# First gate columns of a decoder layer's FFN: low weights meet both token tiles at once, row statistics squared on VectorE

## The chip, the cores and the metric

The kernel runs on one core of one Trainium2 chip. The metric is the device time of one execution in microseconds; several runs are made and their median is compared.

## The reference, cut to what matters

One hybrid decoder layer over 256 tokens of 2048 columns, all float32. Two attention groups share one input projection; their normalised outputs go through one output projection; then comes a GeGLU MLP with a causal depthwise convolution between the up-projection and the activation. The place of the change is the seam between the two sub-layers:

```python
mix = jnp.concatenate([o_a, o_b], axis=-1) @ w_out[l]
x = x + rmsnorm(mix, post_mix_g[l])
h = rmsnorm(x, pre_ffn_g[l])
u = causal_dwconv(h @ w_up[l], conv_w[l], conv_b[l])
gate, val = jnp.split(u, 2, axis=-1)
y = (jax.nn.gelu(gate, approximate=True) * val) @ w_down[l]
```

So the mean square of a whole row of `mix` (2048 columns) must be known before that row's residual can be formed, and the whole residual row is needed, transposed, before the first columns of `h @ w_up` are complete.

## The kernel before, in words

**Tiles.** Tokens are two tiles of 128 rows (0 and 1). A matmul operand is kept as a high part in a reduced format and a low part, the rest; a product is high times high, high times low and low times high. `hT` holds the FFN's input transposed: for each of 16 k tiles of 128 columns, 256 columns with the high part of both token tiles and 256 with the low part. A matmul of high weights streams high and low input together (512 columns for both token tiles, or 2 x 128 for one); a matmul of low weights streams the high input alone (256 columns for both tiles, 128 for one).

**Weights** come in units of 512 KB. The SP queue loads a unit into one of five `raw` buffers, ScalarE casts it to the high part (L95, L112), VectorE subtracts that from `raw` to make the low part (L98, L115). The low split is the last reader of `raw`, so it frees the buffer for the load five units later. A projection of 256 columns takes four units of four k tiles each. `proj_T4` multiplies the high parts of units one and two, their low parts, the low parts of units three and four, and the high parts of these last.

**The seam.** The output projection's last 1024 columns (column blocks 2 and 3) are made tile by tile. A block is added to `mix` on VectorE (`evac_b`, L736), squared and summed on ScalarE (L737) and multiplied by the gain on GpSimd (L738). When all of a tile's sums are there, `mix_rstd` reduces them on VectorE and raises to -0.5 on GpSimd (L183); four `residual` steps on VectorE (L756) make the residual row. `turn` transposes 512 columns of it on PE (L763), writes the high parts of `hT` on ScalarE (`high`, L768) and the low parts on VectorE (`low`, L773). Tile 0 is finished while PE still multiplies tile 1's last output columns.

**`first_gate`** multiplies the first 256 gate columns in two passes, tile 0 while tile 1's residual row is made, then tile 1. Its four weight units are split ahead of it (`gate_unit`); `lows` holds the low splits of units two, three and four, which are called where the code puts them. Before the change, the low weights of units one and two meet tile 0 and tile 1 apart (128 columns each, L928), those of units three and four meet both together (256 columns, L928).

**What sets the order.** PE runs in the order of the program throughout. ScalarE, VectorE and GpSimd run in the order of the program from the output projection's last blocks to the end of `first_gate`; work outside it (casts and splits of the following units, the convolution) is placed into their queues by a scheduler when the program is built. After `first_gate` come the first 256 value columns (`proj_T4`), then the second 256 gate columns, and beside these the convolution of the finished columns: ScalarE copies (L897), VectorE adds (L898), GpSimd multiplies with the row factors `rowf` (L899), ScalarE and VectorE apply the three taps (L901, L903, L905), ScalarE the activation, VectorE the product with the value columns (L1075) and the sums for later use (L958 to L961). The row factors need the FFN's row statistics: squares of the residual rows on ScalarE (L782), a diagonal on VectorE (L203), a matmul that spreads it (L209) and a copy (L866).

Of the kernel before, what the change touches and what calls it, by code (L numbers as in the profile page):

```python
# [8 lines left out]
F32 = mybir.dt.float32  # L9
F32R = mybir.dt.float32r  # L10
BF16 = mybir.dt.bfloat16
AF = mybir.ActivationFunctionType
ALU = mybir.AluOpType
# [4 lines left out]
P = 128  # L18
# [13 lines left out]
def hybrid_layer(ctx: ExitStack, tc: tile.TileContext, x, pre_mix_g, w_in, b_forget, sinks,  # L32
# [282 lines left out]
    with tc.tile_pool(name="mixp", bufs=1) as mp:  # L315
# [416 lines left out]
        def evac_b(t, n, b, h=None):  # L732
            i, cs = (n, slice(0, 512)) if h is None else (4 if h else n,
                                                          slice(h * 256, h * 256 + 256))
            m = mix[t][n][:, cs]
            dve.scalar_tensor_tensor(m, b[:, cs], rstd_b[t], m, op0=ALU.mult, op1=ALU.add)  # L736
            act.activation(junk[:, cs], m, AF.Square, accum_out=msq[t][:, i:i + 1])  # L737
            pool.tensor_tensor(m, m, gbc[:, n * 512:(n + 1) * 512][:, cs], op=ALU.mult)  # L738
# [10 lines left out]
        def mix_rstd(t):  # L749
            st = small.tile([P, 1], F32, tag="st", name="st_m")  # L750
            dve.tensor_reduce(st, msq[t][:, 0:4 + t], axis=AX.X, op=ALU.add)
            rmix.append(rstd_of(st, D, f"rmix{t}"))

        def residual(t, n):
            xs = x_sb[:, t, n * 512:(n + 1) * 512]
            dve.scalar_tensor_tensor(xs, mix[t][n], rmix[t], xs, op0=ALU.mult, op1=ALU.add)  # L756

        def turn(t, n):

            tb = bank("att")  # L760
            for j in range(4):
                c = n * 512 + j * P
                pe.transpose(tb[:, j * P:(j + 1) * P], x_sb[:, t, c:c + P], ident)  # L763
            kts = [(n * 4 + j, tb[:, j * P:(j + 1) * P]) for j in range(4)]

            def high():
                for kt, b in kts:
                    act.activation(hT[:, kt, t * P:(t + 1) * P], b, AF.Copy,  # L768
                                   scale=gcol[:, 16 + kt:17 + kt])

            def low():
                for kt, b in kts:
                    dve.scalar_tensor_tensor(hT[:, kt, 256 + t * P:256 + (t + 1) * P], b,  # L773
                                             gcol[:, 16 + kt:17 + kt],
                                             hT[:, kt, t * P:(t + 1) * P].bitcast(F32),
                                             op0=ALU.mult, op1=ALU.subtract)

            return high, low
# [6 lines left out]
        def out_cols(n, t, cs):  # L785
            b = bank()
            for k, hi, lo in kept[n]:
                mm3(b[:, cs], oT[8 + k], t, hi, lo, cs, k == 0, k == 7)
            return b
# [40 lines left out]
        lows[0]()  # L830
        for _, low in turns:
            low()
        evac_b(1, 2, out_cols(2, 1, slice(0, 256)), 0)
        lows[1]()
        turns = [turn(0, 2), turn(0, 3)]
        for high, _ in turns:
            high()
        turns[0][1]()
        evac_b(1, 2, out_cols(2, 1, slice(256, 512)), 1)
        turns[1][1]()  # L840
        mix_rstd(1)
        for n in range(4):
            residual(1, n)
        hold.__exit__(None, None, None)

# [1 line left out]
    with tc.tile_pool(name="ffn", bufs=1) as fp:  # L847
# [61 lines left out]
        def first_gate():  # L909

            banks = [bank(), bank()]

            def one(t, u):
                ts = slice(t * P, t * P + P)

                both = u >= 2
                ls = slice(0, 256) if both else ts

                def v(x):
                    return x.rearrange("p (h t c) -> p h t c", h=2, t=2)[:, :, t, :]  # L920

                for low in (False, True)[:1 if both and t == 0 else 2]:
                    for kt in range(u * 4, u * 4 + 4):
                        hi, lo = gate[kt]
                        for m, b in enumerate(banks):
                            ms = slice(m * P, (m + 1) * P)
                            if low:
                                pe.matmul(b[:, 256 + ls.start:256 + ls.stop], lo[:, ms],  # L928
                                          hT[:, kt, ls], start=False,
                                          stop=(t == 1 and kt == KT - 1))  # L930
                            else:
                                pe.matmul(v(b), hi[:, ms], v(hT[:, kt, :]),  # L932
                                          start=(t == 0 and kt == 0), stop=False)

            one(0, 0)
            one(0, 1)
            one(0, 2)
            for high, low in [turn(1, u) for u in range(4)]:
                high()
                low()  # L940
            one(0, 3)
            lows[2]()
            x_squares(0)
            x_squares(1)
            for t in range(2):
                act.dma_start(x_dram[t * P:(t + 1) * P, :], x_sb[:, t, :])
            rows = ffn_tables()
            for u in range(4):
                one(1, u)
            later(1, rows)  # L950
            return banks

# [294 lines left out]
```

## Time and profile before

| what | value |
|---|---|
| median of 3 runs | 1063.57 us (1063.05, 1063.57, 1065.51) |
| span of the profiled execution | 1062.6 us; no other time is listed for it |
| mean granted TensorE clock | 0.996 |
| busy: PE, VectorE, ScalarE, GpSimd | 1049.6, 839.7, 639.1, 229.3 us |
| the seam, 333.2 to 348.0 us: PE, VectorE, ScalarE, GpSimd busy | 14.80, 13.27, 10.38, 1.43 us of 14.80 |

Times are microseconds from the span's start. PE, DVE, ACT, POOL and SP are TensorE, VectorE, ScalarE, GpSimd and the DMA queue of SyncE. A row of the timeline has start, length, engine, line, operation, operands and count, and in brackets the idle time before it and what ended it. Successive instructions of an engine overlap a little, so a row's length is somewhat more than what it adds. The chain of waits goes by ends, so its rows for PE start 0.16 us later than the same work in the timeline.

### The profile page before, as it was taken

The numbers are of one execution on the slowest core, as the hardware profiler recorded it, in microseconds if no ns is written. First come the engines' busy times: TensorE is split into PE (matmuls) and PEld (weight loads), VectorE is DVE, ScalarE is ACT, GpSimd is POOL, SyncE is SP. The second block draws the span as 40 slices with busy tenths as digits, with TensorE's granted clock in tenths as the row PEclk, the third lists the DMA queues.
The fourth block names the chain that finished last, engine by engine and source line by source line (L and its number), as shares of the span: only waits on it lengthen the run. The fifth ranks groups of instructions, "written<-read, shape, count | busy, mean of one in ns | idle before, by whom it ended". The sixth has DMA issues, their size and how long they took to land.

```text
span 1062.6 us, 16272 instructions
## 1 busy us (share of the span) xinstructions
PE 1049.6 (99%) x5890; PEld 914.6 (86%) x5890; DVE 839.7 (79%) x1369; ACT 639.1 (60%) x1096; POOL 229.3 (22%) x256
## 2 busy tenths in 40 slices
PE   9999999999999999999999999999999999999996
PEld 7889988888889888888888888888888888888885
DVE  5988887887467887787767999668778687789987
ACT  6767667776556765566655556446556565556551
POOL 4253335441022121211212000002121121200004
PEclk9999999999999999999999999999999999999998
DMA  8745566555773876656665666666566665656563
GB/s 280 217 120 168 162 209 202 165 170 162 282 236 107 280 231 187 193 180 185 211 188 188 193 204 206 213 196 190 169 209 188 197 197 180 194 179 200 194 242 121
DMA packets 154285, 207.08 MB, mean 195 GB/s; under 512 B 6845, under 2 KB 131037, under 8 KB 153181
## 3 DMA queue, kind: packets, MB, share of 16 engines
q1 hardware_dynamic: 153200, 203.37, 60.7%
q10 hardware_dynamic: 1004, 2.68, 0.6%
q8 instruction: 46, 0.75, 0.3%
q14 instruction: 35, 0.28, 0.1%
HBM read 201.68 MB, written 4.21 MB: 194 GB/s over the span
## 4 chain that ended last, share of the span: by engine, by line
PE 84%; DVE 9%; issue 2%; DMA 2%; ACT 2%; POOL 1%; DVEq 0%; SPq 0%; POOLq 0%; ACTq 0%
PE bank_acc L284 15%; PE bank_att L284 14%; PE bank_acc L309 12%; PE bank_att L967 9%; PE bank_acc L290 8%; PE bank_att L290 7%; PE bank_acc L253 7%; DVE wlo L313 4%; PE bank_acc L258 4%; PE bank_acc L967 2%; PE bank_att L475 1%; PE bank_att L510 1%; DVE wlo L115 1%; PE bank_acc L932 1%; DMA raw<-in_w_down_dram 1%
## 5 line engine op out<-in xcount | busy, mean ns | idle before, releaser
L115 DVE TENSOR_TENSOR wlo<-raw,whi 128x1024 fp32r<-128x1024 f32 (+3 forms) x271 | 328.5, 1224 | 127.0 <-ACT whi L112 118.4
L112 ACT CAST whi<-raw 128x1024 fp32r<-128x1024 f32 (+3 forms) x270 | 273.2, 1029 | 131.8 <-issue 88.8
L899 POOL TENSOR_TENSOR room<-room,rowf 128x256 f32<-128x256 f32 x88 | 100.3, 1160 | 393.9 <-DVE room L898 392.0
L284 PE MATMUL bank_acc<-hT,whi 128*128 128x512 f32 x736 | 173.3, 390 | 0.0
L284 PEld LDWEIGHTS bank_acc<-hT,whi 128*128 128x128 f32 x736 | 136.4, 188 | 27.4
L967 PE MATMUL bank_att<-whi,G 128*128 128x512 f32 x488 | 156.0, 389 | 0.0
L284 PE MATMUL bank_att<-hT,whi 128*128 128x512 f32 x640 | 150.6, 390 | 0.0
L284 PEld LDWEIGHTS bank_att<-hT,whi 128*128 128x128 f32 x640 | 118.7, 188 | 23.9
L967 PEld LDWEIGHTS bank_att<-whi,G 128*128 128x128 f32 x488 | 91.6, 188 | 18.9
L967 PE MATMUL bank_att<-wlo,G 128*128 128x512 f32 x244 | 95.0, 389 | 0.2 <-DVE wlo L313 0.2
L290 PEld LDWEIGHTS bank_acc<-hT,wlo 128*128 128x128 f32 x736 | 89.3, 188 | 2.0
L290 PE MATMUL bank_acc<-hT,wlo 128*128 128x256 f32 x736 | 89.8, 279 | 0.0
L901 ACT ACTIVATE room<-room,cw 128x256 f32<-128x256 f32 x88 | 53.0, 602 | 60.6 <-POOL room L899 60.6
L253 PE MATMUL bank_acc<-hT,whi 128*128 128x512 f32 x352 | 88.0, 395 | 0.0
L309 PE MATMUL bank_acc<-whi,oT 128*128 128x512 f32 (+1 forms) x272 | 81.7, 379 | 0.0
L290 PEld LDWEIGHTS bank_att<-hT,wlo 128*128 128x128 f32 x640 | 77.6, 188 | 1.7
L290 PE MATMUL bank_att<-hT,wlo 128*128 128x256 f32 x640 | 77.9, 279 | 0.0
L903 DVE SCALAR_TENSOR_TENSOR room<-room,cw 128x256 f32<-128x256 f32 x88 | 62.4, 709 | 17.6 <-ACT room L901 17.3
L253 PEld LDWEIGHTS bank_acc<-hT,whi 128*128 128x128 f32 x352 | 63.3, 188 | 11.5
L313 DVE TENSOR_TENSOR wlo<-raw,whi 128x1024 fp32r<-128x1024 f32 (+1 forms) x56 | 61.3, 1119 | 12.1 <-ACT whi L312 12.1
L312 ACT CAST whi<-tb 128x1024 fp32r<-128x1024 f32 x42 | 44.0, 1050 | 43.0 <-PE bank_att L967 19.6
L312 ACT CAST whi<-raw 128x1024 fp32r<-128x1024 f32 (+1 forms) x56 | 52.3, 958 | 27.1 <-PE bank_att L967 20.6
(254 smaller groups left out, 1594.0 us busy)
## 6 DMA issues: line engine op xcount, KB each, us to landing
raw<-in_w_up_dram SPq DMA_DIRECT2D x176, 512.0 KB, 4.2
raw<-in_w_down_dram SPq DMA_DIRECT2D x58, 512.0 KB, 4.7
raw<-in_w_in_dram SPq DMA_DIRECT2D x51, 512.0 KB, 4.7
raw<-in_w_out_dram SPq DMA_DIRECT2D x32, 512.0 KB, 4.6
extra<-in_w_down_dram SPq DMA_DIRECT2D x20, 512.0 KB, 4.7
raw<-in_w_in_dram SPq DMA_DIRECT2D x16, 384.0 KB, 3.6
tb<-in_w_down_dram SPq DMA_DIRECT2D x10, 512.0 KB, 3.5
cb<-c_dram SPq DMA_DIRECT2D x8, 256.0 KB, 3.8
```

What stands on the lines that cost most here:

```text
L112: i1 = act.copy(hi[:, cs], raw[:, cs])
L115: i2 = dve.tensor_tensor(lo[:, cs], raw[:, cs], hi[:, cs].bitcast(F32), op=ALU.subtract)
L253: pe.matmul(b, parts[u][0][:, a, m * P:(m + 1) * P], hT[:, kt, :], start=(kt == 0), stop=(kt == KT - 1))
L284: pe.matmul(b, parts[u][0][:, a, m * P:(m + 1) * P], hT[:, kt, :], start=(kt == 0), stop=(kt == KT - 1))
L290: pe.matmul(b[:, 256:512], parts[u][1][:, a, m * P:(m + 1) * P], hT[:, kt, 0:256], start=False, stop=False)
L309: pe.matmul(b, a, r[:, cols], start=(first and i == 0), stop=(last and i == 2))
L312: act.copy(hi, src)
L313: dve.tensor_tensor(lo, src, hi.bitcast(F32), op=ALU.subtract)
L899: pool.tensor_tensor(u[:, 2:258], u[:, 2:258], rowf, op=ALU.mult)
L901: act.activation(y, u[:, 2:258], AF.Identity, bias=cw[:, 3, ch:ch + 1], scale=cw[:, 2, ch:ch + 1])
L903: dve.scalar_tensor_tensor(y, u[:, 1:257], cw[:, 1, ch:ch + 1], y, op0=ALU.mult, op1=ALU.add)
L967: pe.matmul(b[:, to] if to else b, a, r[:, cols], start=(first and i == 0), stop=(last and i == 2))
```

## The change

In `first_gate`, tile 0 now meets the high weights alone. All low weights meet both tiles together, 256 columns at a time, each unit's right behind its high weights' pass over tile 1. Tile 1's transposes move: blocks 0 and 1 ahead of tile 0's fourth high unit, blocks 2 and 3 behind it. The low splits of gate units three and four move behind tile 1's low parts of blocks 2 and 3.

In the row statistics of tile 1, ScalarE squares the first half of column block 2 between the high parts of tile 0's blocks 2 and 3; the sums so far are reduced on VectorE into `v`; the second half is added, then squared and summed on VectorE (`tensor_tensor_reduce`, an operation that the kernel has elsewhere in another form, L481), and the power follows on GpSimd. The gain of that half is multiplied on GpSimd behind the power, and the residual of block 2 is made last.

```diff
+        def mix_others():
+            st = small.tile([P, 1], F32, tag="st", name="st_m")
+            dve.tensor_reduce(st, msq[1][:, 0:4], axis=AX.X, op=ALU.add)
+            v = small.tile([P, 1], F32, tag="rv", name="rv")
+            dve.tensor_scalar(v, st, 1.0 / D, EPS, op0=ALU.mult, op1=ALU.add)
+            return v
+        def square_b(t, n, h):
+            m = mix[t][n][:, h * 256:h * 256 + 256]
+            act.activation(junk[:, 0:256], m, AF.Square, accum_out=msq[t][:, n:n + 1])
+            pool.tensor_tensor(m, m, gbc[:, n * 512 + h * 256:n * 512 + h * 256 + 256],
+                               op=ALU.mult)
...
-        evac_b(1, 2, out_cols(2, 1, slice(0, 256)), 0)
-        lows[1]()
+        b12 = out_cols(2, 1, slice(0, 256))
+        dve.scalar_tensor_tensor(mix[1][2][:, 0:256], b12[:, 0:256], rstd_b[1], mix[1][2][:, 0:256],
+                                 op0=ALU.mult, op1=ALU.add)
         turns = [turn(0, 2), turn(0, 3)]
-        for high, _ in turns:
-            high()
-        turns[0][1]()
-        evac_b(1, 2, out_cols(2, 1, slice(256, 512)), 1)
-        turns[1][1]()
-        mix_rstd(1)
-        for n in range(4):
+        turns[0][0]()
+        square_b(1, 2, 0)
+        turns[1][0]()
+        for _, low in turns:
+            low()
+        v = mix_others()
+        b12 = out_cols(2, 1, slice(256, 512))
+        m12 = mix[1][2][:, 256:512]
+        dve.scalar_tensor_tensor(m12, b12[:, 256:512], rstd_b[1], m12, op0=ALU.mult, op1=ALU.add)
+        ms = small.tile([P, 1], F32, tag="rv", name="ms")
+        dve.tensor_tensor_reduce(junk[:, 256:512], m12, m12, 1.0 / D, v, ALU.mult, ALU.add, ms)
+        r12 = small.tile([P, 1], F32, tag="rmix1", bufs=2, name="rmix1")
+        pool.tensor_tensor(r12, ms, mhalf, op=ALU.pow)
+        rmix.append(r12)
+        pool.tensor_tensor(m12, m12, gbc[:, 1280:1536], op=ALU.mult)
+        for n in (0, 1, 3, 2):
             residual(1, n)
...
-            one(0, 0)
-            one(0, 1)
-            one(0, 2)
-            for high, low in [turn(1, u) for u in range(4)]:
+            def v(x, t):
+                return x.rearrange("p (h t c) -> p h t c", h=2, t=2)[:, :, t, :]
+            def highs(t, u):
+                for kt in range(u * 4, u * 4 + 4):
+                    for m, b in enumerate(banks):
+                        pe.matmul(v(b, t), gate[kt][0][:, m * P:(m + 1) * P], v(hT[:, kt, :], t),
+                                  start=(t == 0 and kt == 0), stop=False)
+            def both_low(u):
+                for kt in range(u * 4, u * 4 + 4):
+                    for m, b in enumerate(banks):
+                        pe.matmul(b[:, 256:512], gate[kt][1][:, m * P:(m + 1) * P],
+                                  hT[:, kt, 0:256], start=False, stop=(kt == KT - 1))
+            for u in range(3):
+                highs(0, u)
+            turns = [turn(1, 0), turn(1, 1)]
+            highs(0, 3)
+            turns += [turn(1, 2), turn(1, 3)]
+            for high, _ in turns:
                 high()
+            for n, (_, low) in enumerate(turns):
                 low()
-            one(0, 3)
-            lows[2]()
+                if n > 1:
+                    lows[n - 1]()
...
             for u in range(4):
-                one(1, u)
+                highs(1, u)
+                both_low(u)
```

**PE, the first gate columns.** L932 is the high weights' pass in the old file and L942 in the new one, L928 and L948 the low weights', L763 and L776 the transposes. Before:

```order
L932 MATMUL bank_acc<-hT_3638,whi 128x2x128 x8
L928 MATMUL bank_acc<-hT_3638,wlo 128x128 x8
L932 MATMUL bank_acc<-hT_3638,whi 128x2x128 x8
L928 MATMUL bank_acc<-hT_3638,wlo 128x128 x8
L932 MATMUL bank_acc<-hT_3638,whi 128x2x128 x8
L763 MATMUL bank_att<-ident,x_sb 128x128 x16
L932 MATMUL bank_acc<-hT_3638,whi 128x2x128 x16
L928 MATMUL bank_acc<-hT_3638,wlo 128x128 x8
L932 MATMUL bank_acc<-hT_3638,whi 128x2x128 x8
L928 MATMUL bank_acc<-hT_3638,wlo 128x128 x8
L932 MATMUL bank_acc<-hT_3638,whi 128x2x128 x8
L928 MATMUL bank_acc<-hT_3638,wlo 128x256 x8
```

Two further runs follow these, eight high and eight low of 256 columns. The changed program:

```order
L942 MATMUL bank_acc<-hT_3638,whi 128x2x128 x24
L776 MATMUL bank_att<-ident,x_sb 128x128 x8
L942 MATMUL bank_acc<-hT_3638,whi 128x2x128 x8
L776 MATMUL bank_att<-ident,x_sb 128x128 x8
L942 MATMUL bank_acc<-hT_3638,whi 128x2x128 x8
L948 MATMUL bank_acc<-hT_3638,wlo 128x256 x8
L942 MATMUL bank_acc<-hT_3638,whi 128x2x128 x8
L948 MATMUL bank_acc<-hT_3638,wlo 128x256 x8
L942 MATMUL bank_acc<-hT_3638,whi 128x2x128 x8
L948 MATMUL bank_acc<-hT_3638,wlo 128x256 x8
```

One further pair of runs follows. Four runs of eight 128-column low matmuls are gone and two runs of eight 256-column ones have come; the first transposes of tile 1 stand behind 24 matmuls instead of 40.

**VectorE, second gate columns beside the convolution.** The numbers tell units apart. In the old program `wlo_4358` is the fourth unit of the second gate columns and `wlo_4412` the first of the second value columns:

```order
L115 TENSOR_TENSOR wlo_4358<-raw_4355,whi_4357 128x1024
L903 SCALAR_TENSOR_TENSOR room_3939<-room_3939,cw_3937 128x256 x2
L905 SCALAR_TENSOR_TENSOR room_3939<-room_3939,cw_3937 128x256 x2
L1075 TENSOR_TENSOR room_3939<-room_3939 128x256 x2
L959 TENSOR_TENSOR s_4296<-room_3939 128x128
L958 TENSOR_TENSOR s_4296<-room_3939 128x128
L115 TENSOR_TENSOR wlo_4412<-raw_4409,whi_4411 128x1024
```

In the new program `wlo_4337` is the third unit of the second gate columns and `wlo_4343` the fourth:

```order
L115 TENSOR_TENSOR wlo_4337<-raw_4334,whi_4336 128x1024
L926 SCALAR_TENSOR_TENSOR room_3939<-room_3939,cw_3937 128x256 x2
L928 SCALAR_TENSOR_TENSOR room_3939<-room_3939,cw_3937 128x256 x2
L1095 TENSOR_TENSOR room_3939<-room_3939 128x256 x2
L979 TENSOR_TENSOR s_4281<-room_3939 128x128
L978 TENSOR_TENSOR s_4281<-room_3939 128x128
L115 TENSOR_TENSOR wlo_4343<-raw_4340,whi_4342 128x1024
```

The convolution's steps stand where they stood; every unit's split stands one place later among them. The casts on ScalarE moved the same way: four of the units' casts stood ahead of the convolution's first tap behind `first_gate`, and now three do.

**SP.** The load of the first value columns' fourth unit stood eighth of the w_up loads, ahead of two loads for w_down; it now stands behind these two. Its buffer is freed by the low split of gate unit three, which is one of the two splits that moved.

More of the change, by code (lines that the diff above doesn't have):

```diff
@@ L911, in first_gate @@
             banks = [bank(), bank()]
[L913 to L933, printed above, removed]
-            one(0, 0)
-            one(0, 1)
-            one(0, 2)
-            for high, low in [turn(1, u) for u in range(4)]:
+            def v(x, t):
[16 more added lines that the diff above has]
+            for high, _ in turns:
                 high()
+            for n, (_, low) in enumerate(turns):
                 low()
-            one(0, 3)
-            lows[2]()
+                if n > 1:
+                    lows[n - 1]()
             x_squares(0)
```

## Prediction

> **What bounds the kernel now.** The page comes first: PE is busy for nearly the whole span.
>
> ```profile
> PE 1049.6 (99%) x5890; PEld 914.6 (86%) x5890; DVE 839.7 (79%) x1369; ACT 639.1 (60%) x1096; POOL 229.3 (22%) x256
> ```
>
> So a change here gains only what PE no longer has to do, and loses whatever PE has to wait. Next, the chain of waits around the seam: start, length, what.
>
> ```profile
> 333.40 0.96 PE bank_acc L932 x8
> 334.36 0.84 PE bank_acc L928 x8
> 335.20 0.99 PE bank_acc L932 x8
> 336.19 0.84 PE bank_acc L928 x8
> 337.03 1.00 PE bank_acc L932 x8
> 338.03 1.75 PE bank_att L763 x16
> 339.78 1.91 PE bank_acc L932 x16
> 341.69 0.84 PE bank_acc L928 x8
> ...
> 343.53 0.84 PE bank_acc L928 x8
> ...
> 345.37 0.94 PE bank_acc L928 x8
> ```
>
> It is PE from end to end: nothing that the other engines do at the seam is late. The price of a run is read directly: eight low matmuls of 128 columns take 0.84 us, eight of 256 columns 0.94 us, eight high ones about 0.97 us, eight transposes 0.87 us.
>
> **PE's work.** Four runs of 0.84 go (3.36), two of 0.94 come (1.88); high runs and transposes are as many as before. PE saves 1.48 us. That is 0.14% of the time, so even all of it lies within 0.2% (2.1 us), about what this measurement can tell from no change.
>
> The Trainium skill (TensorE: Matmul & The Clock Gate, Back-to-back issue gap) gives a sustained 81 ns for a matmul of 128 columns and 131 ns for 512; an estimate on a straight line between is 98 ns for 256, so the merge would save 32 x 81 - 16 x 98 = 1.02 us and the forecast below would be 0.5 higher. The rows, 105 and 118 ns, decide.
>
> **The wait for tile 1's residual.** PE starts the high runs at 333.23 in the timeline; the transposes of tile 1 now come behind three of them, 0.96 + 0.99 + 1.00 later, at 336.2, where before they came at 337.9. What makes the residual row:
>
> ```profile
> 333.69 0.47 DVE L736 SCALAR_TENSOR_TENSOR mix_sb<-bank_acc,rg,mix_sb 128x256 f32<-128x256 f32 x1
> 334.08 1.12 DVE L773 SCALAR_TENSOR_TENSOR hT<-bank_att,gcol,hT 128x128 fp32r<-128x128 f32 x4
> 335.11 0.15 DVE L751 TENSOR_REDUCE st_m<-msq 128x1 f32<-128x5 f32 x1
> 335.29 0.15 DVE L181 TENSOR_SCALAR rv<-st_m 128x1 f32<-128x1 f32 x1
> 336.11 2.74 DVE L756 SCALAR_TENSOR_TENSOR x_sb<-mix_sb,rmix,x_sb 128x512 f32<-128x512 f32 x4 [0.66 <-POOL rmix L183]
> ```
>
> ```profile
> 329.49 1.04 PE L763 MATMUL bank_att<-ident,x_sb 128*128 128x128 f32 x8
> 331.07 0.42 ACT L737 ACTIVATE junk<-mix_sb 128x256 bf16<-128x256 f32 x1 [1.39 <-DVE mix_sb L736]
> 331.48 2.16 ACT L768 ACTIVATE hT<-bank_att,gcol 128x128 fp32r<-128x128 f32 x8
> 335.53 0.55 POOL L183 TENSOR_TENSOR rmix<-rv,mhalf 128x1 f32<-128x1 f32 x1
> ```
>
> In the new order ScalarE's first four high parts start when four transposes are done (329.49 + 4 x 0.11 + the pipeline's 0.2, so 330.2) and end at 331.3; the half square follows to 331.7, the other four high parts to 332.7. VectorE's four low parts behind the last of these end at 333.9 (1.12), reduce and scale at 334.2, the addition of the second half at 334.65 (0.47). The new square and sum has a neighbour in L481:
>
> ```profile
> L481 DVE DVE_READ_ACCUMULATOR2_ANT nm<- x64: 72/83/86, 47.2 to 253.0; 128x1 f32 x64
> L481 DVE CUSTOM_DVE_ANT_0 p<-bank_att,p x32: 259/340/426, 165.5 to 252.7; 128x256 f32<-128x256 f32 x16, 128x128 f32<-128x128 f32 x16
> ```
>
> This trace has it on other operands only, between 0.26 and 0.43; I take 0.43, the longest, and 0.08 for the readout, so 335.2. The power (0.55) ends at 335.75 and the first residual starts at 335.8, 0.3 earlier than 336.11, while PE asks 1.7 earlier. And the gain multiplication now stands right behind the power on GpSimd, beside that residual. The end of the program has this very pair, a 128x256 multiplication behind a power and the step that waits for the power:
>
> ```profile
> 1055.54 0.72 POOL L1154 TENSOR_TENSOR last<-y_sb,gbc_ffn 128x256 f32<-128x256 f32 x1
> ...
> 1055.61 1.20 DVE L1173 SCALAR_TENSOR_TENSOR y_sb<-y_sb,ry,x_back 128x512 f32<-128x512 f32 x1 [0.66 <-POOL ry L1169]
> ```
>
> 1.20 instead of the 0.75 that one of four in L756's row takes. The first residual ends at 337.0, and PE starts the transposes at 337.1: a wait of 0.9. The second ends 0.66 later, 0.2 after PE is through with the first four. Together 1.1 us; without the collision 0.6; with a square of 0.1 more 1.2.
>
> The Trainium skill (SBUF — State Buffer, Who interferes with whom) says that a VectorE instruction with two SBUF inputs and a GpSimd instruction that reads SBUF shut each other out for a whole instruction. By that the residual would lose the 0.65 us left of the multiplication, 0.2 more than the row's 0.45, and PE's wait would be 1.3.
>
> **The rest of the seam** is close, but I cost it at nothing.
>
> ```profile
> 335.55 1.29 ACTq L850 DMA_DIRECT2D cst<-in_conv_w_dram  x3
> 336.87 0.38 ACTq L851 DMA_DIRECT2D cst<-in_conv_b_dram  x1
> 338.51 4.25 ACT L768 ACTIVATE hT<-bank_att,gcol 128x128 fp32r<-128x128 f32 x16 [3.81 <-PE bank_att L763]
> ```
>
> ScalarE issues these four loads before the high parts. They waited for the last gain multiplication on GpSimd and still do; that now ends at 336.45, so they run to 338.2 (1.7). Four high parts end at 339.4, the four low parts on VectorE begin at 339.5, and PE reaches the high run that needs them at 340.0: 337.75 for the second transposes, + 0.44, a high run 0.97, eight transposes 0.87. Half a microsecond later on ScalarE would show on PE. Behind that PE asks for a block every 1.9 us (0.97 + 0.94) and VectorE makes one in 1.06; the splits of gate units three and four, 1.2 each, fit between. The seam ends 1.48 - 1.1 = 0.4 us earlier.
>
> **Where it is lost.** The last row of the rows below is PE at the second gate columns; the others are VectorE's splits beside the convolution.
>
> ```profile
> 353.86 0.64 PE L209 MATMUL bank_att<-diag,ones 128*128 128x128 f32 x4
> 357.57 2.82 DVE L115 TENSOR_TENSOR wlo<-raw,whi 128x1024 fp32r<-128x1024 f32 x2
> 362.22 1.31 DVE L115 TENSOR_TENSOR wlo<-raw,whi 128x1024 fp32r<-128x1024 f32 x1
> 366.00 0.76 DVE L1075 TENSOR_TENSOR room<-room 128x256 f32<-128x256 f32 x2
> 367.07 1.22 DVE L115 TENSOR_TENSOR wlo<-raw,whi 128x1024 fp32r<-128x1024 f32 x1
> 363.50 3.90 PE L290 MATMUL bank_att<-hT,wlo 128*128 128x256 f32 x32
> ```
>
> Before, the split at 362.22 is the fourth unit's and the one at 367.07 belongs to the next projection. By the order, the third now stands in the first place and the fourth in the second, behind the products. Casts and convolution steps stand as before, and this chain begins with the row factors, that is with L209 on PE, so it comes 0.4 earlier, no more. The fourth unit's low part is ready at 367.07 + 1.22 - 0.4 = 367.9. PE needs it at the 25th of the 32 low matmuls: 363.50 + 24 x 0.117 = 366.3 before, 365.9 now. PE waits 2.0 and, with 0.1 for the handover that the transposes showed, starts at 368.0, 1.6 to 1.7 later than before. Each 0.1 of PE's waits at the seam moves the end by 0.1: + 0.5 with none of them, + 2.1 with 0.5 more. Nothing is late next:
>
> ```profile
> 364.67 2.93 ACT L112 CAST whi<-raw 128x1024 fp32r<-128x1024 f32 x3
> ```
>
> The first of these three casts is now the fourth unit's, the others the following projection's; they end by 367.6, and PE wants them behind the fourth unit's high run, at 368.0 + 8 x 0.117 + 3.9 or so, 372.
>
> **The sum**: - 1.48 + 1.1 + 2.0 = + 1.6 us on the span of 1062.6, so 1064.2, 0.15% longer. The median of the runs stands 0.97 above that span, and I add the same to it: 1063.57 + 1.6 = 1065.2.
>
> **The rivals.** First, the gain stays. If VectorE's order let the fourth split through ahead of the products, PE would not wait for it: 1063.57 - 0.4 = 1063.2, and 1062.1 without the waits at the seam. For it: VectorE has idle gaps among these rows.
>
> ```profile
> 364.80 0.48 DVE L903 SCALAR_TENSOR_TENSOR room<-room,cw 128x256 f32<-128x256 f32 x1 [0.39 <-ACT room L901]
> ```
>
> Against: the order is fixed, and the engine takes its instructions in it.
>
> Second, over the bound on the slow side, by a load. The first value columns' fourth unit:
>
> ```profile
> 301.94 30.61 SPq L69 DMA_DIRECT2D raw<-in_w_up_dram  x8
> raw<-in_w_up_dram SPq DMA_DIRECT2D x176, 512.0 KB, 4.2
> gbc_mix<-in_post_mix_g_dram SPq DMA_DIRECT2D x1, 1024.0 KB, 7.9
> 347.90 1.03 ACT L112 CAST whi<-raw 128x1024 fp32r<-128x1024 f32 x1
> 353.25 0.29 DVE L203 TENSOR_SCALAR diag<-ident,rffn 128x128 f32<-128x128 f32 x1 [0.66 <-POOL rffn L183]
> ```
>
> Its load was the eighth of that row, issued at 332.2. Now it waits for the split of gate unit three, which stands behind four residuals and twelve low parts, and is issued at about 343.8. Its cast ran at 347.90, and the squares follow from which the row factors come (L203). ScalarE reaches this cast at 348.4 now: 0.4 earlier with the seam, and I allow 0.9 for one square more ahead of it, about two of the 0.42 of L737's row. A landing within 4.6 us costs nothing (the median is 4.2), and 0.9 more is slack: the diagonal comes about 1.0 earlier, since one cast of 1.03 fewer stands ahead of it, so at 352.25 + 0.29, and PE asks for L209 at 353.86 - 0.4. Beyond 5.5 us each microsecond is one of the total; from 6.0 on it is over 0.2%, and at the 7.9 of the 1 MB load it is + 4.0, 1067.6. For it: it has lost eleven microseconds of lead. Against: it is the first of its burst.
>
> Third, the merge saves less than the rows say, as by the page's figures: + 0.5, 1065.7. Both shapes stand side by side in this trace, which speaks against it. Fourth, that nothing moves at all: the order shows otherwise.
>
> **How the numbers follow.** The forecast has 0.64: 0.50 within 0.2% and 0.14 over it, since + 1.6 with its bounds of + 0.5 and + 2.1 lies 0.5 from the limit and the three runs are 2.5 apart. The kept gain has 0.16, of which 0.03 faster; the late load 0.12, of which 0.10 slower; the smaller saving 0.04, half of it slower; what I don't see 0.04, half faster, half slower. Faster 0.05, within 0.2% 0.67, slower 0.28. The range runs from 1062.6, between the two forms of the kept gain, to 1067.6, the late load's time; the forecast's own is 1064.1 to 1065.7, widened by the runs to 1063.3 and 1067.0.
>
> **What would show it.** PE: transposes L776 with a wait of about 0.9 at 337 that ends with the residual L769; the high run over tile 1 without a longer one; the first value columns at 347.6 instead of 348.0. Then the one row that decides: L290 into bank_att with idle time of 2 us before it, released by VectorE's L115, and L115 standing behind L1095 and L978. If that idle time is not there, the forecast is wrong and the time is 1063 or less. If the cast of the first value columns' fourth unit waits for its load, the second rival is at work.

## The result, and the profile after

The changed kernel takes 1067.20 us (median of 8 runs, 1066.41 to 1068.07) beside 1063.86 of the kernel before (8 runs): a ratio on record of 1.0026, 95% interval 1.0017 to 1.0035. That is 2.8 us more (1.8 to 3.7); the two medians are 3.3 apart, which the interval covers too. So the changed kernel is slower, where + 1.6 us was forecast; the estimate lies over 0.2% (2.1 us), the lower end of its interval does not.

The waits of PE in the changed kernel (for what, how much in all, how often, the longest), of which the kernel before had neither of the two shown:

```profile
PE bank_att L290 <- DVE wlo L115: 1.9, 1, 1.9
...
PE bank_att L776 <- DVE x_sb L769: 0.7, 1, 0.7
```

Both stand where the prediction has them. The timeline of PE at the second gate columns, first before (behind the low run at 363.50, shown in the prediction):

```profile
367.23 7.45 PE L284 MATMUL bank_att<-hT,whi 128*128 128x512 f32 x32
374.52 1.68 PE L290 MATMUL bank_att<-hT,wlo 128*128 128x256 f32 x13
```

then after:

```profile
361.97 2.96 PE L290 MATMUL bank_att<-hT,wlo 128*128 128x256 f32 x24
366.82 1.40 PE L290 MATMUL bank_att<-hT,wlo 128*128 128x256 f32 x8 [1.89 <-DVE wlo L115]
368.02 8.92 PE L284 MATMUL bank_att<-hT,whi 128*128 128x512 f32 x32
376.78 1.45 PE L290 MATMUL bank_att<-hT,wlo 128*128 128x256 f32 x11
```

The low run takes 6.05 us to the next start instead of 3.73, and the 32 high matmuls behind it, in which nothing waits, 8.76 instead of 7.29. What PE waits for is VectorE in its order:

```profile
364.48 0.75 DVE L1095 TENSOR_TENSOR room<-room 128x256 f32<-128x256 f32 x2
365.15 0.28 DVE L979 TENSOR_TENSOR s<-room 128x128 f32<-128x128 f32 x1
365.35 0.28 DVE L978 TENSOR_TENSOR s<-room 128x128 f32<-128x128 f32 x1
365.55 1.22 DVE L115 TENSOR_TENSOR wlo<-raw,whi 128x1024 fp32r<-128x1024 f32 x1
```

And why the matmuls behind the wait are slow is read from the windows of the changed kernel (stretch and length; busy time and count of PE, PEld, DVE, ACT and POOL; the granted clock of PE; the DMA share and GB/s):

```profile
367.00:368.00 1.00, 1.00 (x8) 1.00 (x9) 1.00 (x4) 0.64 (x1) 0.00 (x0) 0.84 0.11 25
368.00:371.00 3.00, 3.00 (x9) 2.34 (x8) 3.00 (x5) 0.62 (x1) 0.00 (x0) 0.50 0.81 252
371.00:372.00 1.00, 1.00 (x6) 0.80 (x5) 0.85 (x1) 0.46 (x1) 0.00 (x0) 0.95 0.94 309
```

The clock falls to half at about 367.68 (0.84 is 0.68 at full and 0.32 at half) and is back at 371.10: 3.42 us. In the kernel before it is 1.00 throughout these windows. In the stream without a wait the last eight low matmuls would have taken 0.93 from start to next start, not 1.20, and the high ones 7.29: 0.27 + 1.47 = 1.74 us lost behind the wait. Some 0.1 of this is not the clock's, since behind a wait at full clock the eight take 1.03 to 1.05 (the runs with zeros below); half of the 3.42 us is 1.71. No term of the prediction had that.

The seam in the chain of waits, after:

```profile
334.53 1.22 DVE x_sb L769
335.76 0.04 issue
335.80 0.66 PE bank_att L776 x4
336.46 0.00 issue
336.46 0.66 PE bank_att L776 x4
337.12 0.96 PE bank_acc L942 x8
338.07 0.87 PE bank_att L776 x8
338.95 1.12 PE bank_acc L942 x8
340.07 0.93 PE bank_acc L948 x8
```

From the first high run to the first value columns it lasted, in PE's timeline, before

```profile
333.23 1.12 PE L932 MATMUL bank_acc<-hT,whi 128*128 128x256 f32 x8
348.04 1.31 PE L284 MATMUL bank_acc<-hT,whi 128*128 128x512 f32 x5
```

14.81 us, and after

```profile
332.06 3.04 PE L942 MATMUL bank_acc<-hT,whi 128*128 128x256 f32 x24
346.52 2.67 PE L284 MATMUL bank_acc<-hT,whi 128*128 128x512 f32 x11
```

14.46: 0.35 less. So the change itself makes - 0.35 + 2.05 (the 25th low matmul was due at 361.97 + 24 x 0.1165 = 364.77 and starts at 366.82) + 1.74 = + 3.4 us in this execution. The two spans differ by 3.2. Two differences outside the change nearly cancel: the changed kernel's execution reaches the seam 1.17 earlier, since its first matmuls took less time (before, then after; the granted clock is printed as 1.00 for both, so why is open),

```profile
6.40 2.05 PE L221 MATMUL bank_att<-hT,whi 128*128 128x512 f32 x4
```

```profile
6.01 1.18 PE L221 MATMUL bank_att<-hT,whi 128*128 128x512 f32 x4
```

and from 376.78 to the end it loses 0.94 again, nearly all in VectorE's last chain, where one addition takes 1.65 instead of 0.69 (before, then after):

```profile
1040.03 0.69 DVE L1128 TENSOR_TENSOR y_sb<-s,y_sb 128x512 f32<-128x512 f32 x1
```

```profile
1042.40 1.65 DVE L1148 TENSOR_TENSOR y_sb<-s,y_sb 128x512 f32<-128x512 f32 x1
```

Neither belongs to the change: the first matmuls take 2.06 in one version with the change too (transposes later), this addition takes 0.69 in seven of the twelve profiles of this document and 1.29 to 1.73 in the other five, with and without PE's wait, and the eight executions of the kernel before are spread over 3.4 us. That is why the seam is compared by its own length below and not by the span.

### The profile page after: what moved, and what is told of

Same layout as the page of the kernel before. It is cut to its first block, busy times and chain, and to the rows that moved or that the text cites. A ratio compares the mean times of both kernels' runs of the same rounds, so it can differ in the third digit from the quotient of the medians.

```text
span 1065.8 us, 16237 instructions
## 1 busy us (share of the span) xinstructions
PE 1049.0 (98%) x5874; PEld 912.5 (86%) x5874; DVE 841.2 (79%) x1371; ACT 638.5 (60%) x1094; POOL 228.4 (21%) x256
## 4 chain that ended last, share of the span: by engine, by line
PE 82%; DVE 10%; issue 2%; ACT 2%; DMA 2%; POOL 1%; SPq 0%; DVEq 0%; POOLq 0%; ACTq 0%
PE bank_acc L284 15%; PE bank_att L284 13%; PE bank_acc L309 12%; PE bank_att L987 9%; PE bank_acc L290 8%; PE bank_acc L253 7%; PE bank_att L290 7%; DVE wlo L313 4%; PE bank_acc L258 4%; PE bank_acc L987 2%; PE bank_att L475 1%; PE bank_att L510 1%; DVE wlo L115 1%; DMA x_in<-in_x_dram 1%; DMA raw<-in_w_down_dram 1%
## 5 line engine op out<-in xcount | busy, mean ns | idle before, releaser
L290 PEld LDWEIGHTS bank_acc<-hT,wlo 128*128 128x128 f32 x736 | 89.3, 188 | 2.0
L290 PE MATMUL bank_acc<-hT,wlo 128*128 128x256 f32 x736 | 89.9, 279 | 0.0
L290 PEld LDWEIGHTS bank_att<-hT,wlo 128*128 128x128 f32 x640 | 77.8, 188 | 3.8 <-DVE wlo L115 2.1
L290 PE MATMUL bank_att<-hT,wlo 128*128 128x256 f32 x640 | 78.4, 280 | 1.9 <-DVE wlo L115 1.9
```

The costliest lines, as they stand in the source:

```text
L290: pe.matmul(b[:, 256:512], parts[u][1][:, a, m * P:(m + 1) * P], hT[:, kt, 0:256], start=False, stop=False)
```

## The experiments

Theory A: PE's idle time before the fourth low part costs twice, once as a wait and once as a half clock behind it. Rivals: the half clock was an accident or contention (B); the loss is elsewhere (C). Later runs ask which part of the change makes the wait, and what else the seam could keep. Ratios are to the kernel before on the same chip; idle time, half clock and seam (from the first high run to the first value columns) are from the one profile of each (the windows from 360 to 376 us, and PE's timeline). The six kernels with the change's own seam have it at 14.27 to 14.46, so a difference of 0.2 between two seams shows nothing. The expectations reckon with the medians' 3.3 us for the change, the table with the ratio's 2.8.

| run | ratio, 95% interval | PE idle before L290, us | clock at half, us | seam, us |
|---|---|---|---|---|
| the change | 1.0026 (1.0017 to 1.0035) | 1.89 | 3.42 | 14.46 |
| early splits | 0.9994 (0.9986 to 1.0003) | none | none | 14.38 |
| 16 zero matmuls | 1.0016 (1.0007 to 1.0025) | none listed | none | 14.28 |
| 8 zero matmuls | 1.0012 (1.0003 to 1.0020) | 0.94 | none | 14.29 |
| 4 zero matmuls | 1.0012 (1.0003 to 1.0021) | 1.43 | none | 14.29 |
| longer wait | 1.0056 (1.0042 to 1.0069) | 3.89 | 6.84 | 14.27 |
| early splits, gain on VectorE | 0.9989 (0.9981 to 0.9998) | none | none | 14.07 |
| the same, transposes later | 0.9990 (0.9982 to 0.9999) | none | none | 13.92 |
| merge alone | 1.0003 (0.9994 to 1.0012) | 0.62 | none | 14.23 |
| statistics alone | 1.0000 (0.9991 to 1.0009) | none | none | 15.09 |
| merge and moved splits | 1.0019 (1.0010 to 1.0028) | 1.90 | 3.42 | 14.24 |

### Early splits: the wait taken away

```diff
-                    proj_T4(w_up, c0, bg)
+                    proj_T4(w_up, c0, bg, made1 if half == 0 and g == 1 else None)
+                if half == 0 and g == 0:
+                    made1 = {u: w_split(w_load(w_rows(w_up, u * 4, 4, 256, 256), 4, 256),
+                                        still=True) for u in range(4)}
```

`proj_T4` takes the units that are made and makes the others.

> The changed kernel with one edit: the four units of the second gate columns are split ahead of the convolution's first tap in VectorE's order, so the fourth unit's low part cannot stand behind the products any more. PE's work and the seam are as in the changed kernel. Theory A (the 1.89 us row before the 25th low matmul makes two costs, the wait itself, about 2.05 us from need to start, and the half clock behind it, granted 0.50 from about 367.8 to 371 us, about 1.6 us): both go, 3.6 us less than the changed kernel, so 0.3 to 0.4 us below the kernel before (about 1063.4), no idle time before L290 into bank_att and a granted clock of 1.00 in all windows from 360 to 376. Theory B (the half clock was an accident of the profiled execution and has nothing to do with the wait): only about 2 us go, so 1.2 to 1.4 above the kernel before, and a half clock may still be seen there. Theory C (the loss is elsewhere, in the seam or in transfers): the time stays 3.3 above.

0.9994 of the kernel before, 0.6 us less (from 1.5 less to 0.3 more), and one row for the whole place, with PE busy throughout and the clock at 1.00:

```profile
360.00:376.00 16.00, 16.00 (x101) 14.36 (x100) 15.26 (x28) 15.09 (x25) 5.68 (x5) 1.00 0.71 235
```

With the wait the half clock goes too. Theory A's number lies in the interval, B (1.2 to 1.4 above) and C (3.3 above) outside it; that the seam's gain is left fits, but so would no gain at all. So the whole loss hangs on the place of these splits: all four were moved, and PE had waited for the fourth.

### Zeros in the wait: PE kept busy, the split as late as it was

```diff
         for kt in range(8, 16):
+            if kt == 12:
+                for i in range(fill):
+                    pe.matmul(banks[i % 2][0:120, 256:512], zero, hT[:, 0, 0:256],
+                              start=False, stop=False)
             low(kt)
```

The zeros are written once, by GpSimd, when the room for the convolution is made; `fill` is 16, 8 or 4 for the second gate columns.

> The changed kernel, where PE multiplies 16 times by a block of zeros (120 rows, 256 columns, into the same accumulators, 16 x 0.117 = 1.87 us) ahead of the 25th low matmul of the second gate columns. The fourth split comes when it came, so the wait's end stays at about 366.8 us, but PE is idle for only about 0.2 us. Theory A (idle time of PE lowers the clock): no half clock behind it, 1.6 us less than the changed kernel, 1.6 to 1.8 above the kernel before. Theory B (accident, or contention of the loads that run at 368 to 371 us): the matmuls behind the wait stay slow in most executions and the time stays 3.3 above the kernel before.

> The same with 8 such matmuls (0.93 us), so that PE is idle for about 1.1 us. If the clock falls only for an idle time longer than that (0.70 us at the seam did not lower it), the result is that of 16: 1.6 to 1.8 above the kernel before. If 1.1 us is enough, 3.3 above as the changed kernel; if it depends on where the idle time falls, executions of both kinds and something between.

> The changed kernel with 4 multiplications by zeros ahead of the 25th low matmul (0.47 us), so that PE is idle for about 1.4 us, between the 0.94 that left the clock at 1.00 and the 1.89 that halved it. If the clock follows the idle share of fixed stretches of about 3.4 us, 1.4 us lies within one of them in most executions: either the limit is above 41% (1.4 of 3.42) and the time is that of 8 or 16 such matmuls, 1.2 to 1.7 above the kernel before with a clock of 1.00, or it is below and the time is 2.8 above as in the changed kernel, with one stretch of 3.42 us at 0.50.

With 16, no idle time is listed (some 0.2 us is left, 2.06 from start to start less 16 x 0.117):

```profile
365.67 2.05 PE L303 MATMUL bank_att<-hT,zero 128*120 128x256 f32 x16
367.73 1.20 PE L290 MATMUL bank_att<-hT,wlo 128*128 128x256 f32 x8
```

The split ends the wait as late as ever, and 1.7 us over the kernel before remain (0.7 to 2.7). With 8 and with 4 it is 1.3 (0.3 to 2.1 and 0.3 to 2.2), and these are the rows of the 25th low matmul, 8 zeros first, then 4:

```profile
367.25 1.20 PE L290 MATMUL bank_att<-hT,wlo 128*128 128x256 f32 x8 [0.94 <-DVE wlo L115]
```

```profile
367.14 1.21 PE L290 MATMUL bank_att<-hT,wlo 128*128 128x256 f32 x8 [1.43 <-DVE wlo L115]
```

In all three profiles the clock stays at 1.00, and the eight matmuls take 1.20 or 1.21, not 1.40 (windows with 16 zeros, with 8 and with 4):

```profile
360.00:376.00 16.00, 15.99 (x94) 14.03 (x93) 15.36 (x26) 11.69 (x20) 4.82 (x4) 1.00 0.79 255
```

```profile
360.00:376.00 16.00, 15.06 (x88) 13.13 (x87) 15.19 (x27) 11.71 (x19) 4.81 (x4) 1.00 0.76 238
```

```profile
360.00:376.00 16.00, 14.57 (x84) 12.66 (x83) 15.15 (x27) 11.68 (x19) 4.82 (x4) 1.00 0.76 236
```

These kernels differ from the change in the zeros and so in PE's idle time at this place; the loads behind the wait still run (the DMA share from 370 to 371 is 0.87, 0.76 and 0.68). So idle time is what lowers the clock, and the accident or contention of rival B falls. The proof is the clock more than the time: B's 3.3 lies outside all three intervals, but the change's own interval (1.8 to 3.7) overlaps them. 1.43 us left the clock alone where 1.89 halved it, in one profile each. With 4 zeros two of the eleven executions took 1067.9 and 1068.0, the others 1065.0 to 1065.7; whether the clock fell in these two is not known. That it is about the same total for 0.2, 0.94 and 1.43 us of idle time is what a wait of fixed end must give: filling it is free.

### A longer wait

```diff
+            for _ in range(twice):
+                dve.tensor_tensor(lo[:, cs], raw[:, cs], hi[:, cs].bitcast(F32), op=ALU.subtract)
             i2 = dve.tensor_tensor(lo[:, cs], raw[:, cs], hi[:, cs].bitcast(F32), op=ALU.subtract)
```

`twice` is 1 for the fourth unit of the second gate columns.

> The changed kernel, where the fourth unit's low part is made twice: the first time where it stood, the second time behind the splits of G and one sum, so that PE's wait grows from 2.05 to about 3.9 us (0.76 + 0.29 and twice 1.2 less overlaps). Theory A with a fixed length of the half clock (3.2 us of it, 1.6 lost): 1.9 above the changed kernel, 5.2 above the kernel before. If the half clock's length grows with the idle time: 2.8 or more above the changed kernel, over 6 above the kernel before. Theory B: 1.9 above the changed kernel, with no rule for the clock.

```profile
369.54 2.08 PE L293 MATMUL bank_att<-hT,wlo 128*128 128x256 f32 x8 [3.89 <-DVE wlo L117]
```

```profile
368.00:369.00 1.00, 0.00 (x0) 0.00 (x0) 1.00 (x3) 0.35 (x1) 0.00 (x0) 0.78 0.00 0
369.00:375.00 6.00, 5.46 (x17) 4.68 (x18) 4.70 (x6) 0.62 (x1) 0.00 (x0) 0.50 0.64 194
375.00:376.00 1.00, 1.00 (x5) 0.79 (x4) 0.00 (x0) 0.89 (x1) 0.00 (x0) 0.80 1.00 331
```

6.0 us over the kernel before (4.5 to 7.3), which covers both lengths that were expected; the windows decide. The half clock lasts from 368.56 to 375.40, 6.84 us: two stretches of 3.42. So its length is not fixed; in the three profiles that have it, it is one such stretch or two. The first of the two, 368.56 to 371.98, began while PE was still idle (0.98 us of it), and after it a second one passed before the clock was back. Nor does the fall stand at a fixed distance from the wait: it comes 0.98 us before PE resumes here, 0.86 after it in the changed kernel. The sum of the result's section gives - 0.54 for the seam, + 4.05 for the start of the 25th low matmul and half of the 5.86 us that PE works at half clock, + 2.93: + 6.4, with 6.0 measured.

### Which part makes the wait

The merge alone keeps the old statistics and `lows[1]` in its old place; of the change it has only

```diff
-            for u in range(4):
-                one(1, u)
+            for u in range(4):
+                highs(1, u)
+                both_low(u)
```

with the high runs over tile 0 and the transposes of tile 1 in the new order. (Gate unit four's low split stands behind tile 1's last low part on VectorE in every version, the kernel before included; the only split that the change moves there is unit three's.) In the statistics alone, it is the reverse: the new statistics and the moved splits with the old `one(t, u)`.

> The kernel before with only the new order of PE in the first gate columns (high weights apart, low weights of all units for both tiles together, the transposes moved); the row statistics, ScalarE's squares and the place of the third gate unit's low split are as before, so its load is as early as before. Theory A (PE's shorter work is what pushes the fourth split of the second gate columns behind the products): a wait of 1.5 to 2 us before L290 into bank_att although statistics and load are as before; the seam 0.7 shorter, since the residual comes at 336.1 + 0.75 and is asked for at 336.2. So 0.9 to 1.4 above the kernel before, and 1.6 more where the clock falls, which an idle time of 1.89 us did and one of 0.94 us did not. Rival (the moved splits and the late load cause it): no such wait, 0.7 below the kernel before.

> The kernel before with only the new row statistics of tile 1 and the moved low splits of gate units three and four; PE's order and matmuls are as before. Theory A: the fourth split stands ahead of the products as before, no wait of PE, the residual row is ready about 0.3 us earlier than needed already, nothing is gained: within 0.3 us of the kernel before, although the load of the first value columns' fourth unit is issued eleven microseconds later here too. Rival (the late load or the moved splits cost time): a wait of PE at the first value columns or before L290, 1 to 3.6 above the kernel before.

The merge alone has the wait, but of 0.62 us, not of 1.5 to 2:

```profile
366.31 1.20 PE L290 MATMUL bank_att<-hT,wlo 128*128 128x256 f32 x8 [0.62 <-DVE wlo L115]
```

Theory A's order was right (the fourth split stands behind the products here too) and its size wrong: VectorE took both first taps ahead of the splits, and its last products began 1.23 us after the low run had begun, 2.51 in the changed kernel. The statistics alone change nothing in the time, 1.0000 (0.9991 to 1.0009), late load and moved splits included; PE waits nowhere at the first value columns or before L290. Their seam is 0.28 longer, all of it inside the sixteen transposes (1.95 from start to next start, 1.67 before), so without the merge they gain nothing. Neither part alone makes the wait of 2 us. The last run differs from the merge alone in one place only: gate unit three's low split (`lows[1]()`) stands where the changed kernel has it, behind `low` of tile 1's block 2. The statistics are the old ones.

> The merge alone, with the low splits of gate units three and four where the changed kernel has them, so that the load of the first value columns' fourth unit is late too; the row statistics are the old ones. The merge alone had a wait of 0.62 us before L290, not 1.5 to 2, and its VectorE took the taps of both first convolutions ahead of the splits. Theory A2 (the moved splits, by the later load, set the order of splits and taps that makes the long wait; the merge only puts the fourth split behind the products): the order of VectorE is again that of the changed kernel, so a wait of 1.9 to 2.1 us, a half clock behind it, and 2 to 3.5 above the kernel before. Rival (the new statistics are needed for it): 0.6 us, and no measurable difference from the kernel before.

```profile
366.98 1.86 PE L290 MATMUL bank_att<-hT,wlo 128*128 128x256 f32 x8 [1.90 <-DVE wlo L115]
```

VectorE's order is that of the changed kernel again, the wait is back, and so is a half clock of 3.42 us (the windows print 0.63 from 367 to 368, 0.50 to 370 and 0.66 to 371, so from 367.26 to 370.68, 0.28 behind PE's start); 2.0 us over the kernel before (1.1 to 3.0). The long wait needs the merge and the moved split of unit three together, and not the new statistics. Why the scheduler's order turns on these two is not shown.

This run shows one more thing. Its executions are of two kinds: four with a mean granted clock of 0.997 took 1064.60 to 1064.98 us, five with 0.995 took 1066.39 to 1068.94, and three with 0.996 lay at 1065.36, 1066.56 and 1069.04. A stretch of 3.42 us at half lowers the mean over 1065 us by 0.0016, about the difference of the first two groups (0.002, printed to three places). The program is the same each time; one execution was profiled, one with 0.995, so that the others had the same wait, or no half clock, is not shown. If the clock were set by how long PE was idle within fixed stretches of 3.42 us, the idle time would fall into one stretch in some executions and across the border of two in others. This fits, and so does a fall at no fixed distance from the wait, but it was not seen directly.

### What else the seam could keep

```diff
-        pool.tensor_tensor(m12, m12, gbc[:, 1280:1536], op=ALU.mult)
+        dve.tensor_tensor(m12, m12, gbc[:, 1280:1536], op=ALU.mult)
```

on top of the early splits, and in the second run also

```diff
-        for n in (0, 1, 3, 2):
+        for n in range(4):
             residual(1, n)
...
+            highs(0, 3, 0, 2)
             turns = [turn(1, 0), turn(1, 1)]
-            highs(0, 3)
+            highs(0, 3, 2, 4)
```

> The kernel with the early splits, and the gain of tile 1's last half block is multiplied on VectorE in the 0.66 us that it waits for the power, instead of on GpSimd behind the power. Theory A (GpSimd's multiplication makes the first residual 0.45 us longer, and PE waits for that): the first residual falls from 1.22 to about 0.75 us, PE's wait before the first transposes of tile 1 from 0.70 to 0.25 us, the seam is 0.4 us shorter than with the early splits alone, about 0.8 below the kernel before. Rival (the residual is long for another reason, such as the first read of its operands): length and wait stay at 1.22 and 0.70.

> As before it, and the first transposes of tile 1 stand behind half of tile 0's fourth high unit (4 matmuls, 0.48 us, later), with the residuals in the order of their blocks. Theory A (PE's loss at the seam is only these waits): no wait of PE over 0.1 us at the seam, so that nearly the whole 1.48 us of saved matmul time is kept: from the first high run to the first value columns 13.3 us (14.77 before, 14.46 in the changed kernel), and the total 1.4 below the kernel before, about 0.13%. Rival (the waits only move to the second transposes or to the high run over tile 1): the seam stays at 13.8 us or more.

The gain on VectorE, its chain of waits:

```profile
334.38 0.80 POOL rmix L864
335.18 0.02 issue
335.20 0.76 DVE x_sb L771
335.96 0.04 issue
336.01 0.65 PE bank_att L778 x4
```

The first residual falls from 1.22 to 0.76 us: GpSimd's multiplication had made it longer, as forecast. But the power now takes 0.80 instead of 0.56, with VectorE's multiplication beside it, so half of the gain goes back. The seam is 14.07, 0.3 shorter than with the early splits alone and 0.2 below the shortest with the collision; 0.9989, 1.2 us under the kernel before (0.2 to 2.0), the first version that is shown to be faster.

With the transposes later, no wait at the seam is listed any more, and yet the seam is 13.92, not 13.3 (of 14.81 before, which the expectation has as 14.77). The losses are now inside the groups:

```profile
336.59 1.32 PE L778 MATMUL bank_att<-ident,x_sb 128*128 128x128 f32 x8
337.66 0.72 PE L944 MATMUL bank_acc<-hT,whi 128*128 128x256 f32 x4
338.22 1.04 PE L778 MATMUL bank_att<-ident,x_sb 128*128 128x128 f32 x8
339.20 1.34 PE L944 MATMUL bank_acc<-hT,whi 128*128 128x256 f32 x8
340.38 1.10 PE L950 MATMUL bank_acc<-hT,wlo 128*128 128x256 f32 x8
```

From start to start the first transposes take 1.07 and the second 0.98, where eight without a wait take 0.79 to 0.82, and the high run over tile 1 takes 1.18 instead of 1.02 to 1.03: 0.6 us in all. The rival was right: the losses moved. 0.9990 is the same time as the run before.

## Why the prediction was right or wrong

**PE's work** was right: the eight low matmuls of 256 columns take 0.93 to 0.94 in the changed kernel too, so the third rival, the smaller saving, falls.

**The wait for tile 1's residual** was right in place, cause and size. In the changed kernel

```profile
333.38 0.48 DVE L860 CUSTOM_DVE_ANT_0 junk<-mix_sb,rv 128x256 bf16<-128x256 f32 x1
333.79 0.08 DVE L860 DVE_READ_ACCUMULATOR2_ANT ms<- 128x1 f32 x1
```

the new square takes 0.48 (0.43 taken, the longest of the rows), the readout 0.08, and the residual collides with the gain for 1.22 (1.20 taken). It loses 0.46 to that (0.76 without, in the gain on VectorE), not the 0.65 left of the multiplication. PE's wait is listed as 0.70, counted from the end of the row before it; from when they were due (332.06 + 3 x 0.96 = 334.94) the transposes start 0.86 late, where 0.9 was forecast. The seam is 0.35 shorter; 0.4 was forecast. Merge alone tells what the new statistics gave for it: a seam of 14.23 with the old ones, 14.27 to 14.46 with the new ones and 14.07 without the collision. The collision took back what the earlier square gained.

**The rest of the seam**, costed at nothing, was nearly so: the high run over tile 1 took 1.12 in the chain of this execution, 0.95 in that of the gain on VectorE.

**The fourth split** was right: 2.0 us and 0.1 for the handover forecast, an idle time of 1.89 and a start 2.05 late measured, released by the row that was named. The prediction read the order of VectorE off the program and did not ask what makes it: it takes the merge together with the moved split of gate unit three.

**The late load**, the second rival, did not come to pass: in the changed kernel the cast of the fourth value unit runs at

```profile
347.29 1.04 ACT L112 CAST whi<-raw 128x1024 fp32r<-128x1024 f32 x1
```

without a wait for its load, and the statistics alone, with the same late load, measured 1.0000.

**Where it was wrong** is the sum, "- 1.48 + 1.1 + 2.0 = + 1.6 us". Each of its three terms came out within 0.2 us, and a fourth was missing: what PE's idle time does to the matmuls behind it, + 1.74 us in the profiled execution. The measured + 2.8, and the medians' + 3.3, lie between the sum without it and with it (+ 1.7 and + 3.4). Whether part of the executions escaped the half clock, as the mean clocks suggest for the run of merge and moved splits, cannot be said from the changed kernel's eight; their mean clocks are 0.994 to 0.996. The part of the chance that was given to a time over 0.2%, 0.28, came too low for the same reason, since the bound of + 2.1 was taken from the waits at the seam alone. And it is luck that the range holds the measured time: 1067.20 is over the 1067.0 to which the forecast's own times were widened, and under 1067.6 only because that end was set for the late load, which did not happen.

Two smaller slips, on which nothing hangs: 368.0 + 8 x 0.117 + 3.9 is 372.8, not 372; and 0.97 us was taken for what lies around a span, from a median and a span that are not of one execution. The changed kernel's profiled execution took 1067.55 us with a span of 1065.8, so 1.75 lies around it.

The Trainium skill (TensorE: Matmul & The Clock Gate, What's actually happening) tells of the half clock after a window of about 3.4 us without work, and of windows of 3413 ns that run on by themselves. The lengths of 3.42 and 6.84 us agree with the windows; for the idle time the measurement decides: 1.89 us was enough here.

## What to carry to other kernels

A wait of the engine that bounds the kernel has a second price where its clock follows its use: here 1.9 us of idle time cost up to 1.7 us more, while 1.4 us cost nothing further in its one profile, so a forecast should price a new wait of that size with both. Shortening the bounding engine's work moves what a scheduler places beside it, so the due times of the next stage have to be looked at again; giving the urgent splits their place in the order was worth the whole loss. A multiplication moved off the critical engine can still cost there when the two engines work at the same time; the test is the length of the neighbour's row.

## What the runs showed of the hardware that was not expected

- The granted clock of TensorE goes to 0.50 after an idle time of 1.89 or 1.90 us in an otherwise busy stream, in stretches of 3.42 us: one for 1.89 us, two for 3.89. Idle times of 0.62, 0.70, 0.94 and 1.43 us left it at 1.00, in one profile each or more. The fall came 0.86 and 0.28 us after PE had resumed, and with 3.89 us of idle time 0.98 before.
- One program (merge and moved splits) has executions with mean clocks of 0.997 and of 0.995, at 1064.6 to 1065.0 and 1066.4 to 1068.9 us; the one that was profiled, of the second kind, has one stretch at half clock.
- GpSimd and VectorE slow each other in both directions: a residual of 0.76 us takes 1.22 beside a 128x256 multiplication on GpSimd, and GpSimd's power of one column 0.80 instead of 0.56 beside a 128x256 multiplication on VectorE (in both runs that have it there).
